# A hybrid encoder layer on one core: time steps finished in PSUM, attention outputs fetched earlier, two of eight gates kept in SBUF

## The chip, the core and the metric

The kernel runs on one core of a Trainium2 chip. A core has TensorE (PE in the profile; PEld is its loading of weights), VectorE (DVE), ScalarE (ACT), GpSimd (POOL) and SyncE (SP), which here only issues transfers. Each engine works off its own queue in order; they wait for each other by semaphores. SBUF is the working memory, PSUM holds the eight banks that TensorE writes. The metric is the device time of one execution in microseconds, the median of several; each comparison also has one profiled execution.

## The reference

One layer over 512 tokens of width 1024, float32. What the change touches is the token mixer:

```python
h = rmsnorm(x, pre_mix_norm[l])
proj = h @ w_in[l]                       # 1024 x 9792: z, x/B/C, dt, q, k, v, two gates
z, xbc, dt_raw, q, k, v, gates = split_cols(proj, IN_SPLITS)
# SSD branch, both directions, chunks of 128 tokens:
dt = softplus(dt_raw + dt_bias)          # time steps, 32 heads x 2 directions
a_dt = dt * -exp(a_log); a_cs = cumsum(a_dt) within the chunk
# ... scan with decays exp(a_cs), gated norm by groups, @ w_ssd_out -> y_ssd
# attention branch: +-128 tokens, 16 query heads on 4 key heads, sink logit, T5 bias
y_attn = window_attention(q, k, v, attn_sink[l], rel_bias_table) @ w_attn_out[l]
g = sigmoid(gates + b_gate)              # two gates, 1024 wide each
mixed = (g_ssd * y_ssd + g_attn * y_attn) @ w_o[l]
x = x + rmsnorm(mixed, post_mix_norm[l])
```

Behind it stands an MLP, 1024 to 4096 to 1024 with squared ReLU, with a norm ahead and behind, added to x.

## The kernel before

All of the activations lie transposed, 128 channels by 512 tokens. **Products.** A float32 matmul is made of three in the format float32r: every operand is split into a high part (ScalarE's copy, rounded) and a low part (the rest, a subtraction), and `mm3` sums high by high, high by low and low by high in one bank. A product of 128 columns of a weight matrix (`cm`) loads 512 KB of weights, splits them (line 538 on ScalarE, line 542 in three pieces on GpSimd) and issues 24 matmuls of 128x512. Three buffers each for raw weights, high and low parts stand ahead of TensorE. A product is called a quantum in the code; the list of quanta is the skeleton of the program, and everything else is hung on it: `self.at(q, fn)` says at which quantum `fn` is written out.

**Stages.** First the normed input h is made and split in 16 tiles (lines 758 to 761), v and dt come first, and `dt_math` (line 805 on) makes the time steps: softplus as a series on VectorE and ScalarE in one PSUM bank that holds two tiles, e and s2; line 828 writes the time steps `self.dt`, one of the tables in SBUF that the scan uses; line 830 multiplies them by -exp(a_log) into `al` (tile dtw). Three matmuls sum `al` along the chunk; all decays hang on these. Then nine rounds of input products (x, B, C, z, q and gates) stand between the scan of eight groups, with the sixteen attention heads spread over them. An attention output pair is scaled by VectorE (line 1006) and stored to DRAM (`spill`); so is each gate (`gate_quantum`, line 1043). In the last round the eight attention outputs are fetched (`attn_fetch`), split (`attn_split`, lines 1034 and 1035, the low parts in turn on VectorE and GpSimd) and multiplied by w_attn_out, eight products; each result is multiplied by its fetched gate (line 1051). The products by w_ssd_out, w_o and the MLP follow, from about 590 us to the end.

**Memory.** 83 slots of 128x512 in SBUF hold everything that is not weights. `Slots.get` takes the slot that has been free longest, `put` gives one back. Before the attention products the 16 tiles of h are given back, and the split of the attention outputs takes 16 slots then.

**The order.** When all is written out, `Planner` (line 117 on) makes each engine's order by a list schedule: it has a cost for every instruction (`duration`), a rule that VectorE with two wide SBUF operands and GpSimd hold each other off (`locks`, not for PSUM operands), a due time from the last instruction that needs the result (`deadlines`), and picks on each engine what is ready and due first. The engines' queues are then chained in that order. A small edit can so move instructions on all engines.

Of the kernel before, what the change touches and what calls it, by code (L numbers as in the profile page):

```python
# [14 lines left out]
ALU = mybir.AluOpType  # L15
# [48 lines left out]
            x_flip=1, b_flip=1, x_turn=1)  # L64
LAST = dict(SCAN, prep=(0, 1, 3, 4), outs=(2.5, 5.5), rms=8, finish=11)
FILLED, HEAD0, HEAD1 = "sfssfssfs", 1, -11
HEADS = dict(scores=0, flip=2, values=3.5)
BUCKET_STARTS = (1, 2, 3, 4, 5, 6, 7, 8, 12, 16, 23, 32, 46, 64, 91)

# [28 lines left out]
class Slots:  # L98
# [5 lines left out]
    def get(self, name, shape=(128, 512), dtype=F32):  # L104
        s = self.free.popleft()
        self.n += 1
        t = self.pool.tile(list(shape), dtype, tag=f"s{s}", name=f"{name}_{self.n}", bufs=1)
        self.tags[t.tensor.name] = f"s{s}", 1
        self.slot[id(t)] = (s, t)
        return t  # L110

    def put(self, *tiles):
        for t in tiles:
            self.free.append(self.slot.pop(id(t))[0])
# [287 lines left out]
class Trunk:  # L402
# [89 lines left out]
    def at(self, q, fn):  # L492

        self.acts.setdefault(max(q, self.now), []).append(fn)
# [310 lines left out]
    def dt_math(self):  # L805
        nc = self.nc
        get, put = self.slots.get, self.slots.put
        bias = self.row[:, :128].rearrange("p (i h) -> p i h", i=2)
        self.tables = [get("tables", (128, 2, 4, 64)) for _ in range(3)]
        self.ncs = self.tables[2][:, 0]  # L810
        self.dt, self.cs, self.dec, self.coef = (self.tables[i // 2][:, i % 2] for i in range(4))
        w = [self.dtv] + [get("dtw", (128, 4, 64)) for _ in range(3)]
        v, r, p, al = w
        bank = self.bank("ps")
        e, s2 = (bank[:, a:a + 256].rearrange("p (c h) -> p c h", c=4) for a in (0, 256))

        nc.scalar.activation(r, v, AF.Abs)
        nc.scalar.activation(e, r, AF.Exp, scale=-1.0)
        nc.scalar.activation(r, e, AF.Identity, bias=self.two)
        nc.vector.reciprocal(r, r)  # L820
        nc.vector.tensor_tensor(e, e, r, op=ALU.mult)
        nc.scalar.activation(s2, e, AF.Square)
        nc.scalar.activation(p, s2, AF.Copy, scale=1.0 / 17)
        nc.scalar.activation(v, v, AF.Relu)
        for n in (15, 13, 11, 9, 7, 5, 3):
            nc.vector.scalar_tensor_tensor(p, p, 1.0 / n, s2, op0=ALU.add, op1=ALU.mult)
        nc.vector.scalar_tensor_tensor(s2, p, 1.0, e, op0=ALU.add, op1=ALU.mult)
        nc.vector.scalar_tensor_tensor(self.dt, s2, 2.0, v, op0=ALU.mult, op1=ALU.add)
        nc.scalar.activation(bias[:, 1], bias[:, 1], AF.Exp)
        nc.vector.scalar_tensor_tensor(al, self.dt, -1.0, bias[:, 1].unsqueeze(1).to_broadcast([128, 4, 64]),  # L830
                                       op0=ALU.mult, op1=ALU.mult)

        def sums():
            pc = self.bank("ps")
            pc3 = pc[:, :256].rearrange("p (c h) -> p c h", c=4)
            self.mm(pc3[:, :, 0:32], self.U, al[:, :, 0:32], True, True)
            self.mm(pc3[:, :, 32:64], self.L, al[:, :, 32:64], True, True)
            pt = self.bank("ps")
            self.mm(pt[:, :256], self.ones, al, True, True)
            nc.vector.tensor_copy(self.cs, pc3)  # L840
            nc.scalar.activation(self.ncs, self.cs, AF.Copy, scale=-1.0)
            pt3 = pt[:, :256].rearrange("p (c h) -> p c h", c=4)
            nc.scalar.activation(self.dec, pt3, AF.Exp)
            nc.vector.tensor_tensor(self.coef, pt3, self.cs, op=ALU.subtract)
            nc.scalar.activation(self.coef, self.coef, AF.Exp)
            nc.vector.tensor_tensor(self.coef, self.coef, self.dt, op=ALU.mult)
            put(*w)

        def rows():
            px = self.bank("ps")  # L850
            for c in range(4):
                self.tr(px[:64, c * 128:(c + 1) * 128], self.cs[:, c, :])
            csr, cse = get("csr"), get("cse")
            nc.vector.tensor_copy(csr[:64], px[:64])
            nc.scalar.activation(cse[:64], px[:64], AF.Exp)
            self.csT = self.dp.tile([64, 512], F32, name="csT")
            self.csE = self.dp.tile([64, 512], F32, name="csE")
            chunks = lambda a: a.rearrange("p (c t) -> p c t", c=4)
            nc.sync.dma_start(self.inside(self.csT, 0, [128, 64], [8192, 4], [1, 128]), chunks(csr[:64]))
            for i in range(2):  # L860
                nc.sync.dma_start(self.inside(self.csE, 4096 * i, [128, 32], [8192, 4], [1, 128]), chunks(cse[i:64:2]))
            put(csr, cse)
            self.show("dt", self.dt)
            self.show("cs", self.cs)

        self.later(4, sums)
        self.later(5, rows)
# [154 lines left out]
        return t  # L1022

    def gate_fetch(self, m):
        self.gate[m] = self.fetch(self.gate[m], "gate")

    def attn_fetch(self):
        assert len(self.kept) == 8
        self.kept = [self.fetch(self.kept[k], "a") for k in range(8)]

    def attn_split(self):
        for k, a in enumerate(self.kept):
            hi, lo = self.slots.get("ah", dtype=F32R), self.slots.get("al", dtype=F32R)
            self.nc.scalar.copy(hi, a)
            (self.nc.vector if k % 2 == 0 else self.nc.gpsimd).tensor_tensor(lo, a, hi.bitcast(F32), op=ALU.subtract)
            self.slots.put(a)
            self.at_.append((hi, lo))

    def gate_quantum(self, m, dst):

        def done(ps):
            t = self.slots.get("gate")
            self.nc.scalar.activation(t, ps, AF.Tanh, bias=self.gbias(m), scale=0.5)  # L1043
            dst[m] = self.spill(t)

        return self.cm(self.d_w_in_b, C_GS - 64 + m * 128, lambda: self.h, done)

# [307 lines left out]
    def place_head(self, h, q):  # L1355

        at = lambda d: round(2 * (q + d)) / 2
        self.at(at(-2), lambda: self.attn_bias(h))
        self.at(at(HEADS["scores"]), lambda: self.attn_scores(h))
        self.at(at(HEADS["flip"]), lambda: self.attn_flip(h))  # L1360
        if h % 2:
            self.at(at(HEADS["values"]), lambda: self.attn_values(h // 2) if h // 2 in ALONE else self.due.append(h // 2))

# [461 lines left out]
    def build(self):  # L1825
# [4 lines left out]
        n = lambda: len(self.quanta)  # L1830
# [6 lines left out]
        for g in range(-1, 8):  # L1837
            q0 = n()
            if g < 7:
                f = deque(q[g + 3:g + 4] + ga[g + 1:g + 2] + gs[g + 1:g + 2])  # L1840
                p = deque(self.ssd_quanta(g + 1))
                for k in FILLED:
                    self.add(*[(p if k == "s" else f).popleft()] if k == "s" or f else [])
                if g < 0:
                    a0 = q0
                if g == 6:
                    for h in range(16):
                        self.place_head(h, a0 + HEAD0 + h * (n() + HEAD1 - a0 - HEAD0) / 15)
            else:
                self.at(n() - 4, self.attn_fetch)  # L1850
                self.at(n(), lambda: self.slots.put(*sum(self.h, ())))
                self.at(n(), self.attn_split)
                for m in range(8):
                    self.at(n() - 1, lambda m=m: self.gate_fetch(8 + m))
                    self.add(self.attn_out_quantum(m))
                for m in range(8):
                    self.at(n() - 2 + m // 2, lambda m=m: self.gate_fetch(MIX_ORDER[m]))
            if g >= 0:
                m = n() - q0
                self.place_ssd(g, lambda i, q0=q0, m=m: q0 + (min(i, m + 2) if g == 7 else round(i * m / 4) / 2 if 0 <= i <= 8 else m + i - 8 if i > 8 else i))  # L1860
# [47 lines left out]
```

## Time and profile before

| | us |
|---|---|
| runs, median (lowest to highest) | 1047.94 (1044.93 to 1048.61) |
| profiled execution, its own time | 1050.14 |
| its span, first to last instruction | 1048.4 |
| TensorE busy | 1035.3 |
| VectorE, GpSimd, ScalarE busy | 807.3, 730.0, 661.6 |

The profile's rows name a source line, an engine, an operation, and out<-in by the names of the tiles, with buffer numbers left out: `pp` and `ps` are PSUM banks, `wh` and `wl` the split weights, `h` the split input, `ah` and `al` the split attention outputs, `dtw` the tiles of the time steps' computation. In a timeline the two first numbers are the start and the duration in us, and brackets tell for how long the engine had been idle and what ended that. Matmuls overlap: one of 128x512 is shown as 0.39 long, and the next starts sooner. A table by stretches gives for each engine its busy time there, then the granted share of TensorE's clock, the busy share of the transfer engines and GB/s. Line numbers of the new file are one higher from line 67 on, two higher behind line 828, three behind 1026 and four behind 1850 (the scan's functions so stand three lines lower).

### The profile page before, as it was taken

Reading aid. Unit: us, or ns where it says so; the run is one execution under the profiler, and the core shown is the slowest. Engines: PE = TensorE matmul, PEld = TensorE weight load, DVE = VectorE, ACT = ScalarE, POOL = GpSimd, SP = SyncE. Lnnn points to the kernel's source line nnn. Section 1 sums busy time; section 2 is a strip of 40 time slices with the busy share of each in tenths; the row PEclk is TensorE's granted clock in tenths of the full one; section 3 lists DMA queues with packets and bytes.
Section 4 is the critical chain, followed back from the end, with each engine's and each line's share of the span. In section 5 each row is a group of like instructions: output and inputs, shape, how many; then the busy total and the mean of one; then the engine's idle time right before and its main releaser. Section 6 shows DMA issues by size and latency. Waiting matters only on the chain.

```text
span 1048.4 us, 16447 instructions
## 1 busy us (share of the span) xinstructions
PE 1035.3 (99%) x5298; PEld 867.9 (83%) x5298; DVE 807.3 (77%) x1371; ACT 661.6 (63%) x1393; POOL 730.0 (70%) x800
## 2 busy tenths in 40 slices
PE   9999999999999999999999999999999999999997
PEld 8788888888788888888878888889888888888886
DVE  6886987979989998896999546787853674584697
ACT  7776868775878787876877234656554444434553
POOL 5957567476585756748689655134688898898995
PEclk9999999999999999999999999999999999999999
DMA  8379989799799989999876734236222422424132
GB/s 309 114 185 243 228 233 202 178 224 226 190 243 232 238 178 236 252 228 237 227 205 213 254 124 138 97 110 205 88 89 83 141 81 89 153 80 161 61 101 81
DMA packets 151446, 182.27 MB, mean 174 GB/s; under 512 B 81976, under 2 KB 96312, under 8 KB 151360
## 3 DMA queue, kind: packets, MB, share of 16 engines
q1 hardware_dynamic: 151072, 180.92, 63.7%
q8 instruction: 42, 0.69, 0.3%
q14 instruction: 44, 0.36, 0.1%
q10 hardware_dynamic: 288, 0.30, 0.1%
HBM read 136.81 MB, written 27.59 MB: 157 GB/s over the span
## 4 chain that ended last, share of the span: by engine, by line
PE 47%; DVE 2%; ACT 1%; POOL 1%; DMA 1%; issue 1%; POOLq 0%; SPq 0%; DVEq 0%; ACTq 0%
PE pp L463 24%; PE ps L463 22%; DMA rstd<-rrow 1%; DVE yT L1345 0%; POOL wl L1693 0%; DVE x L1488 0%; DVE acc L1467 0%; POOL x L1819 0%; PE pp L467 0%; PE ps L467 0%; ACT wh L538 0%; DVE m L1240 0%; ACT yh L1388 0%; ACT th L1135 0%; POOL mrs L1481 0%
## 5 line engine op out<-in xcount | busy, mean ns | idle before, releaser
L542 POOL TENSOR_TENSOR wl<-wr,wh 128x342 fp32r<-128x342 f32 (+1 forms) x390 | 392.6, 1021 | 223.4 <-ACT wh L538 213.5
L463 PE MATMUL pp<-h,wh 128*128 128x512 f32 (+1 forms) x1664 | 505.7, 386 | 1.2 <-ACT gate L1043 0.9
L463 PEld LDWEIGHTS pp<-h,wh 128*128 128x128 f32 x1664 | 307.3, 188 | 62.2 <-issue 1.7
L463 PE MATMUL pp<-h,wl 128*128 128x512 f32 (+1 forms) x832 | 320.7, 386 | 0.0
L538 ACT CAST wh<-wr 128x1024 fp32r<-128x1024 f32 (+1 forms) x130 | 134.9, 1038 | 126.9 <-PE pp L463 94.9
L463 PEld LDWEIGHTS pp<-h,wl 128*128 128x128 f32 x832 | 156.8, 188 | 30.9 <-issue 0.2
L1693 POOL TENSOR_TENSOR wl<-wd,wh 128x256 fp32r<-128x256 f32 x158 | 133.4, 881 | 12.5 <-ACT wh L1690 12.1
L1690 ACT CAST wh<-wd 128x512 fp32r<-128x512 f32 x92 | 53.2, 618 | 36.3 <-PE ps L463 20.8
L463 PE MATMUL ps<-wl,fh 128*128 128x512 f32 x184 | 71.8, 390 | 0.2 <-POOL wl L1693 0.2
L463 PE MATMUL ps<-wh,fl 128*128 128x512 f32 x184 | 71.6, 389 | 0.0
L463 PE MATMUL ps<-wh,fh 128*128 128x512 f32 x184 | 71.6, 389 | 0.0
L1528 DVE SCALAR_TENSOR_TENSOR pp<-pp,r 128x256 f32<-128x256 f32 (+1 forms) x31 | 17.3, 558 | 66.7 <-ACT r L1525 66.5
L1237 ACT ACTIVATE n<-cb,tables 128x128 f32<-128x128 f32 x128 | 49.6, 391 | 17.7 <-DVE cb L1228 17.7
L1231 POOL TENSOR_TENSOR rb<-rb,tables 128x512 f32<-128x512 f32 x32 | 38.8, 1218 | 23.3 <-DMA rb<-csT 8.6
L1066 DVE SCALAR_TENSOR_TENSOR u<-pp,cv,u 128x510 f32<-128x510 f32 (+1 forms) x64 | 47.8, 747 | 3.3 <-ACT u L1062 2.0
L1238 ACT ACTIVATE m<-cb,tables 128x128 f32<-128x128 f32 x128 | 49.3, 389 | 0.0
L1233 ACT ACTIVATE rf<-rf,tables 128x128 f32<-128x128 f32 x128 | 41.5, 391 | 8.1 <-DMA rf<-csT 8.1
L463 PEld LDWEIGHTS ps<-wl,fh 128*128 128x128 f32 x184 | 34.5, 188 | 8.0 <-POOL wl L1693 0.6
L463 PEld LDWEIGHTS ps<-wh,fh 128*128 128x128 f32 x184 | 34.5, 188 | 7.2
L463 PEld LDWEIGHTS ps<-wh,fl 128*128 128x128 f32 x184 | 34.6, 188 | 7.1
L943 DVE COPY dp<-P 128x768 uint16<-128x768 uint16 (+1 forms) x48 | 39.7, 848 | 0.3
L973 ACT ACTIVATE P<-P,mx 128x256 f32<-128x256 f32 (+1 forms) x64 | 35.5, 557 | 7.0 <-DVE mx L965 6.8
(299 smaller groups left out, 2197.1 us busy)
## 6 DMA issues: line engine op xcount, KB each, us to landing
wr<-in_w_in_b SPq DMA_DIRECT2D x74, 512.0 KB, 5.2
wr<-in_w_mlp_in_b SPq DMA_DIRECT2D x32, 512.0 KB, 3.5
wd<-in_w_mlp_out SPq DMA_DIRECT2D x64, 256.0 KB, 5.3
zt<-dp SPq DMA_DIRECT2D x40, 256.0 KB, 5.2
rb<-csT SPq DMA_DIRECT2D x32, 256.0 KB, 5.5
rf<-csT SPq DMA_DIRECT2D x32, 256.0 KB, 5.5
wr<-in_w_ssd_out_b SPq DMA_DIRECT2D x13, 512.0 KB, 3.5
zt<-dp SPq DMA_DIRECT2D x32, 192.0 KB, 3.8
```

Of the source, the lines that this page charges most:

```text
L463: self.nc.tensor.matmul(out, lhsT, rhs, start=start, stop=stop, skip_group_check=more)
L538: self.nc.scalar.copy(hi[:, :m], raw)
L542: self.nc.gpsimd.tensor_tensor(lo[:, c], raw[:, c], hi[:, c].bitcast(F32), op=ALU.subtract)
L943: (copy or nc.vector.tensor_copy)(apart.rearrange("p (u k) -> p u k", u=2), src.bitcast(U16)[:, :2 * w].rearrange("p (k u) -> p u k", u=2))
L973: nc.scalar.activation(p[:, :w], p[:, :w], AF.Exp, bias=mx[:, n:n + 1], scale=-1.0, accum_out=sm[:, n:n + 1])
L1066: nc.vector.scalar_tensor_tensor(u[:, a:e], ps[:, a + d:e + d], self.wtap(t, b), u[:, a:e], op0=ALU.mult, op1=ALU.add)
L1231: nc.gpsimd.tensor_tensor(v4(rb), v4(rb), cs[:, 1].unsqueeze(2).to_broadcast([128, 4, 128]), op=ALU.subtract)
L1233: nc.scalar.activation(v4(rf)[:, h], v4(rf)[:, h], AF.Identity, bias=ncs[:, 0, h:h + 1])
L1237: nc.scalar.activation(v4(n)[:, h], cb[:, 0], AF.Copy, scale=dt[:, 0, h:h + 1])
L1238: nc.scalar.activation(v4(m)[:, h], cb[:, 1], AF.Copy, scale=dt[:, 1, h:h + 1])
L1690: nc.scalar.copy(hi, src)
L1693: (nc.vector if q == 512 else nc.gpsimd).tensor_tensor(lo[:, c], src[:, c], hi[:, c].bitcast(F32), op=ALU.subtract)
```

## The change

Three edits. **Time steps in the bank.** The last step of the softplus writes its result over s2 in the PSUM bank; the copy that the tables need is made by ScalarE (line 830 of the new file), and `al` is computed from s2 in PSUM (line 832). **Attention outputs.** They are fetched six products ahead of the first product that uses them, instead of four, and split in two halves, three products ahead and one, where all eight were split right at it. The 24 slots for this are taken while the 16 tiles of h are still held. **Gates.** Of each eight gates the last two (numbers 6, 7, 14 and 15) are neither stored nor fetched; they stay in the slots in which ScalarE made them.

```diff
+SPILLED = 6
@@ dt_math
-        nc.vector.scalar_tensor_tensor(self.dt, s2, 2.0, v, op0=ALU.mult, op1=ALU.add)
+        nc.vector.scalar_tensor_tensor(s2, s2, 2.0, v, op0=ALU.mult, op1=ALU.add)
+        nc.scalar.copy(self.dt, s2)
         nc.scalar.activation(bias[:, 1], bias[:, 1], AF.Exp)
-        nc.vector.scalar_tensor_tensor(al, self.dt, -1.0, bias[:, 1].unsqueeze(1).to_broadcast([128, 4, 64]),
+        nc.vector.scalar_tensor_tensor(al, s2, -1.0, bias[:, 1].unsqueeze(1).to_broadcast([128, 4, 64]),
                                        op0=ALU.mult, op1=ALU.mult)
@@
     def gate_fetch(self, m):
-        self.gate[m] = self.fetch(self.gate[m], "gate")
+        if m % 8 < SPILLED:
+            self.gate[m] = self.fetch(self.gate[m], "gate")
@@
-    def attn_split(self):
-        for k, a in enumerate(self.kept):
+    def attn_split(self, k0):
+        for k, a in enumerate(self.kept[k0:k0 + 4]):
@@ gate_quantum
-            dst[m] = self.spill(t)
+            dst[m] = self.spill(t) if m % 8 < SPILLED else t
@@ build
-                self.at(n() - 4, self.attn_fetch)
+                self.at(n() - 6, self.attn_fetch)
+                self.at(n() - 3, lambda: self.attn_split(0))
                 self.at(n(), lambda: self.slots.put(*sum(self.h, ())))
-                self.at(n(), self.attn_split)
+                self.at(n() - 1, lambda: self.attn_split(4))
```

The planner makes a new order from it. From the first half of the mixer to the last attention products (about 25 to 580 us) it differs on every engine in places; behind that no instruction changes its place. VectorE's queue around the end of the time steps, before (ps_363 is the bank, its wide inputs otherwise lie in SBUF):

```order
L880 TENSOR_TENSOR KL_515<-pp_487,KH_513 128x512
L827 SCALAR_TENSOR_TENSOR ps_363<-dtw_361,ps_363 128x256
L828 SCALAR_TENSOR_TENSOR tables_357<-ps_363,dtw_71 128x256
L830 SCALAR_TENSOR_TENSOR dtw_362<-tables_357,row 128x256
L906 SCALAR_TENSOR_TENSOR pp_533<-pp_533,rb_420 128x512
L915 TENSOR_TENSOR Q_559<-pp_533,Q_559 64x512
```

and now:

```order
L828 SCALAR_TENSOR_TENSOR ps_363<-dtw_361,ps_363 128x256
L882 TENSOR_TENSOR KL_516<-pp_488,KH_514 128x512
L829 SCALAR_TENSOR_TENSOR ps_363<-ps_363,dtw_71 128x256
L908 SCALAR_TENSOR_TENSOR pp_534<-pp_534,rb_421 128x512
L832 SCALAR_TENSOR_TENSOR dtw_362<-ps_363,row 128x256
L917 TENSOR_TENSOR Q_560<-pp_534,Q_560 64x512
```

The key split and the first scaling of a query bank have each traded places with a step of the time steps, and `al` (dtw_362) reads the bank. On TensorE the three sums of `al` stand one matmul sooner than before, ahead of the one that was the last in front of them.

VectorE's queue where the attention outputs are split, before (al is a low half of an attention output, yl one of the scan's output, sl of the squares for its norm):

```order
L1035 TENSOR_TENSOR al_6457<-a_6161,ah_6456 128x512
L1073 SCALAR_TENSOR_TENSOR C_6328<-th_6334,C_6328 128x512
L1035 TENSOR_TENSOR al_6465<-a_6165,ah_6464 128x512
L481 TENSOR_TENSOR sl_6313<-ssq_6303,sh_6312 128x512
L1138 SCALAR_TENSOR_TENSOR z_6382<-th_6384,pp_6357 128x2x128
L1035 TENSOR_TENSOR al_6473<-a_6169,ah_6472 128x512
L1138 SCALAR_TENSOR_TENSOR z_6383<-th_6384,pp_6357 128x2x128
L1138 SCALAR_TENSOR_TENSOR z_6382<-th_6444,pp_6405 128x2x128
L1138 SCALAR_TENSOR_TENSOR z_6383<-th_6444,pp_6405 128x2x128
L1389 TENSOR_TENSOR yl_6658<-yT_2130,yh_6657 128x512
```

and now:

```order
L1038 TENSOR_TENSOR al_6231<-a_6006,ah_6230 128x512
L1285 TENSOR_TENSOR w_5563<-ps_6301,z_5720 128x512
L1177 TENSOR_TENSOR xl_6357<-xd_6354,xh_6356 128x256
L1038 TENSOR_TENSOR al_6239<-a_6010,ah_6238 128x512
L1177 TENSOR_TENSOR xl_6363<-xd_6360,xh_6362 128x256
L1038 TENSOR_TENSOR al_6414<-a_6018,ah_6413 128x512
L1038 TENSOR_TENSOR al_6406<-a_6014,ah_6405 128x512
L482 TENSOR_TENSOR sl_6322<-ssq_6312,sh_6321 128x512
L1141 SCALAR_TENSOR_TENSOR z_6391<-th_6393,pp_6366 128x2x128
L1141 SCALAR_TENSOR_TENSOR z_6392<-th_6393,pp_6366 128x2x128
```

All four low halves that VectorE makes now stand together ahead of sl and of the products by z; before, three stood between these and the fourth fourteen places behind the third. SyncE's queue for the fetches, now:

```order
L1017 DMA sd_5881<-a_5879 128x512
L1023 DMA a_6006<-sd_1697 128x512
L1023 DMA a_6008<-sd_2237 128x512
L1023 DMA a_6010<-sd_3001 128x512
L1023 DMA a_6014<-sd_4065 128x512
L1023 DMA a_6018<-sd_5618 128x512
L519 DMA wr_6164<-in_w_in_b 128x1024
L1216 DMA rb_6424<-csT 128x512
L1023 DMA a_6020<-sd_5881 128x512
L1338 DMA rrow_5925<-rcol_5924 128x4
L1023 DMA a_6016<-sd_4829 128x512
L519 DMA wr_6222<-in_w_attn_out_b 128x1024
```

With one more that stands before these, six fetches are issued ahead of the last load of input weights (wr_6164) and all eight ahead of the first load of w_attn_out here; the last attention output is stored (sd_5881) right before its fellows are fetched.

## The prediction

> **What bounds the kernel now.** I read the page's first part, then the table by stage, then TensorE's own waits, and only then two places in time.
>
> ```profile
> PE 1035.3 (99%) x5298; PEld 867.9 (83%) x5298; DVE 807.3 (77%) x1371; ACT 661.6 (63%) x1393; POOL 730.0 (70%) x800
> ```
>
> ```profile
> core 0: us, PE busy (x) PEld busy (x) DVE busy (x) ACT busy (x) POOL busy (x), PEclk, DMA share, GB/s
> ...
> 600.00:650.00 50.00, 50.00 (x222) 41.43 (x221) 24.85 (x42) 16.00 (x23) 29.03 (x32) 1.00 0.39 128
> ```
>
> TensorE is the bound all through: from 600 us on it is never free (50.00 of 50), so whatever is saved before 600 us reaches the end undiminished, and nothing in the change lies behind that. What can be won is only what TensorE loses in waits and at a low clock. Its longest waits (total, times, longest):
>
> ```profile
> PE ps L463 <- DVE dtw L830: 2.0, 1, 2.0
> PE pp L463 <- DVE al L1035: 1.0, 1, 1.0
> PE pp L463 <- ACT gate L1043: 0.9, 1, 0.9
> ...
> PE ps L463 <- DVE w L1282: 0.3, 1, 0.3
> PE pp L463 <- DVE C L1066: 0.3, 1, 0.3
> PE ps L463 <- DVE mx L965: 0.3, 1, 0.3
> ```
>
> The two longest are the two that the change aims at: L830 makes the product of time step and decay rate (tile dtw, called al in the code), L1035 the low halves of the attention outputs (al).
>
> **Time steps in the bank.** The timeline of VectorE, GpSimd and TensorE at the first wait, and the clock there:
>
> ```profile
> 39.26 0.68 DVE L880 TENSOR_TENSOR KL<-pp,KH 128x512 fp32r<-128x512 f32 x1
> ...
> 40.77 6.23 DVE L830 SCALAR_TENSOR_TENSOR dtw<-tables,row 128x256 f32<-128x256 f32 x1
> 46.93 0.69 DVE L906 SCALAR_TENSOR_TENSOR pp<-pp,rb 128x512 f32<-128x512 f32 x1
> ```
>
> ```profile
> 39.35 3.56 POOL L761 TENSOR_TENSOR h<-xt,h 128x257 fp32r<-128x257 f32 x5
> 42.86 0.92 POOL L542 TENSOR_TENSOR wl<-wr,wh 128x342 fp32r<-128x342 f32 x1
> 43.73 2.13 POOL L761 TENSOR_TENSOR h<-xt,h 128x256 fp32r<-128x256 f32 x3
> 45.81 2.85 POOL L542 TENSOR_TENSOR wl<-wr,wh 128x341 fp32r<-128x341 f32 x3
> ```
>
> ```profile
> 44.65 0.39 PE L463 MATMUL pp<-h,wl 128*128 128x512 f32 x1
> 47.06 0.71 PE L463 MATMUL ps<-dtw,cst 128*128 128x128 f32 x4 [2.02 <-DVE dtw L830]
> ...
> 47.85 1.27 PE L463 MATMUL pp<-h,wh 128*128 128x512 f32 x2
> ...
> 52.38 0.28 PE L463 MATMUL ps<-KH,Q 128*128 128x256 f32 x1
> ```
>
> ```profile
> 44.00:47.00 3.00, 1.04 (x5) 0.54 (x3) 3.00 (x2) 0.00 (x0) 2.92 (x5) 1.00 0.51 175
> 47.00:48.50 1.50, 1.44 (x8) 1.28 (x9) 0.85 (x3) 0.83 (x2) 1.50 (x2) 0.84 0.00 0
> 48.50:51.40 2.90, 2.90 (x8) 2.33 (x7) 2.45 (x5) 2.80 (x5) 2.10 (x4) 0.50 0.53 172
> ```
>
> L830 took 6.23 us. Both its wide operands lie in SBUF, and GpSimd works on SBUF without a pause beside it. That GpSimd is the cause is told by the group ahead of it: L826 is of the same form and size, ran beside a GpSimd that was as busy, but with one operand in PSUM, and seven times it took no more than 423 ns (its duration here as min/median/max, in the first row):
>
> ```profile
> L826 DVE SCALAR_TENSOR_TENSOR dtw<-dtw,ps x7: 421/422/423, 36.2 to 38.9; 128x256 f32<-128x256 f32 x7
> L1035 DVE TENSOR_TENSOR al<-a,ah x4: 683/876/1411, 527.1 to 545.4; 128x512 fp32r<-128x512 f32 x4
> ```
>
> The change gives L830 (L832 in the new file) a PSUM operand, so I price it at 0.42. When is it done? The last L826 starts at 38.9 and ends at 39.3. Behind them the new order puts the closing product (0.42), a key split (L880, 0.68), the time step (0.42), the scaling of a query bank (L906, 0.69) and then this one (0.42): 2.63, so about 42.0 us. TensorE asks for it where it now issues the matmul at 44.65. It is there over 2 us early, and the wait is gone.
>
> What it is worth: before, the score matmuls start at 52.38. Without the wait there stand, after 44.65, one matmul (0.23), the sums (0.80, from 47.06 to 47.85), twelve matmuls of 0.227 (2.72; the stage from 600 us has 222 in 50.00 us, 0.225, and the last two rows of the fence on the attention outputs stand 0.23 apart), and two changes of number format for which I allow 0.3: 48.70. Gain 3.7, in 3.4 to 4.0. About 2.0 of it is the wait and the rest the half clock behind it (0.50 for 2.9 us, 0.84 for 1.5: 1.45 + 0.24 = 1.7 us).
>
> What comes next in line? GpSimd is no slower than before: its low halves of h end at 43.73 + 2.13 = 45.86, and the last is asked for at about 48; its weight piece ends at 48.66, of which the first third (46.7) is asked for at about 50.3. ScalarE gets one more instruction, the copy of the time steps to SBUF:
>
> ```profile
> 47.65 0.58 ACT L914 CAST Q<-pp 64x512 fp32r<-64x512 f32 x1 [5.06 <-DVE pp L906]
> ...
> 52.43 0.38 ACT L843 ACTIVATE tables<-ps 128x256 f32<-128x256 f32 x1
> ```
>
> An instruction of its size from PSUM took 0.38, and ScalarE sat idle for 5.06 us here behind the same late VectorE: I put it at nothing. If the idle time were gone, the query casts would be 0.4 later; the query bank is scaled by 41.6, so even then they are some 6 us ahead of the scores at 48.7.
>
> [...] The row first: L830 lost 5.8 us to about eight GpSimd instructions, while every other VectorE instruction in that position (the second row above, 683 alone and 1411 at most) lost no more than one. [...]
>
> **Attention outputs.** The second wait, in TensorE's and VectorE's timelines:
>
> ```profile
> 528.93 0.39 PE L463 MATMUL pp<-ah,wh 128*128 128x512 f32 x1
> ...
> 531.97 0.39 PE L463 MATMUL pp<-ah,wh 128*128 128x512 f32 x1
> 533.36 0.50 PE L463 MATMUL pp<-al,wh 128*128 128x512 f32 x1 [1.00 <-DVE al L1035]
> ...
> 535.32 0.39 PE L463 MATMUL pp<-ah,wl 128*128 128x512 f32 x1
> 535.55 0.39 PE L463 MATMUL pp<-al,wh 128*128 128x512 f32 x1
> ```
>
> ```profile
> 529.24 1.41 DVE L1035 TENSOR_TENSOR al<-a,ah 128x512 fp32r<-128x512 f32 x1
> 530.58 1.41 DVE L481 TENSOR_TENSOR sl<-ssq,sh 128x512 fp32r<-128x512 f32 x1
> 531.90 0.41 DVE L1138 SCALAR_TENSOR_TENSOR z<-th,pp 128x256 f32<-128x256 f32 x1
> 532.24 1.07 DVE L1035 TENSOR_TENSOR al<-a,ah 128x512 fp32r<-128x512 f32 x1
> ```
>
> From 528.93 to 535.55 start 23 matmuls: 22 distances of 0.227 are 4.99, and it took 6.62. So 1.6 us are lost, because VectorE makes each low half only when TensorE already stands before it. In the new order (rows in the section on the change) all four of VectorE's low halves stand ahead of the y splits and ahead of the ssq split that came between. I take 1.3 of 1.6; the bounds are 1.6 (all) and 0 (the four only trade places with scan work, for which TensorE then waits). The data is no matter: the last fetch was issued at 506.92, 20 us before its use.
>
> ```profile
> 506.92 0.39 SPq L1021 DMA_DIRECT2D a<-sd  x1
> ```
>
> **Fetches earlier, four gates less.** Two products of 24 matmuls are 10.9 us, so eight fetches of 256 KB (2.1 MB) move from the second of these stretches toward the first, and eight transfers of the same size (four spills, four fetches) fall away, the spills mostly in the first:
>
> ```profile
> 449.00:499.00 50.00, 49.95 (x328) 42.60 (x327) 39.15 (x70) 36.20 (x83) 34.07 (x37) 1.00 0.97 234
> 499.00:549.00 50.00, 48.74 (x240) 39.35 (x239) 46.82 (x67) 40.02 (x84) 39.59 (x37) 1.00 0.77 217
> ```
>
> ```profile
> wr<-in_w_in_b SPq DMA_DIRECT2D x74, 512.0 KB, 5.2
> ```
>
> At 234 GB/s the moved 2.1 MB are 9.0 us of transfer, the spills 4.5 less. A weight load lands in 5.2 us (the last row) and three weight buffers hold it two products (10.9) ahead: 5.7 us of cover against 4.5. I put the whole at nothing, bounds 0 and 3.3 (9.0 less 5.7).
>
> **The rest of the order.** The planner moves scan work on all engines up to about 580 us. TensorE's other waits there (gate 0.9; w, C and mx 0.3 each) are 1.8 us; a new order may lose them or find as many. Among what it may find are waits for memory: 24 slots are taken while h holds 16, so scan tiles get slots that were given back more lately. I take 0, bounds 1.8 either way.
>
> **Sum.** 3.7 + 1.3 = 5.0 us. The profiled execution took 1050.14 (span 1048.4), so 1045.1 there; the median of the runs is 2.2 lower, 1047.94, so 1042.9.
>
> **Rivals.**
> 1. The half clock is not in the timed runs. For: the profiled execution is 1.5 us slower than the slowest timed run, about the clock's price. Against: clock and wait stand side by side in the only trace. Then 2.0 + 1.3: 1044.6. [...]
> 2. The attention wait stays: VectorE is 46.82 of 50 busy there, and a split that comes earlier pushes scan work. 3.7 alone: 1044.2.
> 3. The re-planned order also loses the small waits: 3.7 + 1.3 + 1.8 = 6.8: 1041.1.
> 4. L830's 6.23 us is not GpSimd's doing, but for instance the broadcast row operand, which stays. By the row 421/422/423 less likely. Only 1.3: 1046.6. [...]
> 5. Slower: SyncE's queue is in order, and the last input weights and the first attention weights now stand behind six and eight fetches. If nothing covers them, TensorE stops for 9.0 and runs 1.7 longer at half clock: +10.7 - 3.7 = +7.0: 1054.9. It decides once such a load lands over 5.7 us late. Against: the four gates' traffic is gone from the same queue.
>
> **How the numbers follow.** Forecast 0.49, rival 1 0.14, 2 0.11, 3 0.16, 4 0.06, 5 0.04. 0.5% is 5.2 us here, about what can be told from no change, and the bound is 1042.7, close to the forecast: of its 0.49, which spreads over 1041.1 to 1044.7 with the unknown order, I count 0.25 below and 0.24 above. Faster: 0.25 + 0.16 = 0.41. Slower: 0.04. Same: the rest, 0.55. The range reaches from rival 3 with all bounds at their best (4.0 + 1.6 + 1.8 = 7.4, 1040.5) to rival 4 (1046.6), each with some 0.5 more for the spread of a median: 1040.0 to 1047.2.
>
> **What would show it.** Right: L832 takes about 0.42 us; no TensorE wait on dtw; the clock 1.00 from 44 to 52; the first score matmul near 48.7; 23 matmuls of the first attention product within 5.3 us; the end 5 us sooner with TensorE still 50.00 of 50 from 600 us. Wrong: L832 still long; half clock elsewhere; a wait on al, on a weight load or on scan work between 480 and 580 us that was not there.

## The result: 0.37% faster, at the time that was forecast, but not from where it was forecast

| | us |
|---|---|
| forecast | 1042.9 (1040.0 to 1047.2) |
| after, median of 7 runs (lowest to highest) | 1042.79 (1040.58 to 1043.83) |
| before, beside it, 7 runs | 1046.54 (1044.85 to 1048.61) |
| ratio, 95% interval | 0.9963 (0.9947 to 0.9978) |
| after, profiled execution (its span) | 1043.74 (1042.0) |

The page's first part of the changed kernel, and all the waits that TensorE has in it (total, times, longest):

```profile
PE 1032.8 (99%) x5298; PEld 868.6 (83%) x5298; DVE 794.0 (76%) x1371; ACT 662.4 (64%) x1394; POOL 728.8 (70%) x800
```

```profile
PE ps L464 <- ACT xh L1176: 1.1, 1, 1.1
PE pp L464 <- PEq L1900: 0.8, 1, 0.8
PE ps L464 <- DVE xl L1177: 0.5, 1, 0.5
```

That is within 0.5%, the likeliest of the three cases by the forecast. The gain, 3.75 us, is three quarters of the 5.0 that were forecast. The waits on the time steps, on the attention halves and on the gate are gone (those on the time steps and the gate are missing from the second profile of the kernel before as well, further down); the waits on the scan's x halves (xh, xl) are 1.6 us where they were 0.4. At the time steps everything stands as forecast. VectorE's and TensorE's timelines there, and the table by stretches:

```profile
40.05 0.69 DVE L908 SCALAR_TENSOR_TENSOR pp<-pp,rb 128x512 f32<-128x512 f32 x1
41.14 0.42 DVE L832 SCALAR_TENSOR_TENSOR dtw<-ps,row 128x256 f32<-128x256 f32 x1 [0.39 <-ACT tables L830]
```

```profile
48.83 0.28 PE L464 MATMUL ps<-KH,Q 128*128 128x256 f32 x1
...
411.93 0.39 PE L464 MATMUL ps<-xh,bt 128*128 128x256 f32 x1 [1.08 <-ACT xh L1176]
412.81 0.39 PE L464 MATMUL ps<-xl,bt 128*128 128x256 f32 x1 [0.49 <-DVE xl L1177]
```

```profile
48.50:51.40 2.90, 2.90 (x18) 2.55 (x17) 2.42 (x9) 1.92 (x4) 2.82 (x5) 1.00 0.49 177
...
410.00:414.00 4.00, 2.43 (x13) 1.65 (x12) 3.13 (x5) 2.99 (x6) 4.00 (x7) 1.00 1.00 377
414.00:417.50 3.50, 3.50 (x11) 2.73 (x10) 2.86 (x4) 2.99 (x9) 3.42 (x4) 0.51 1.12 218
```

L832 took 0.42 and ended at 41.56, the clock behind it is 1.00, and the first score matmul stands at 48.83. But a new stop with a new half clock stands at 410 to 417.5.

To see where time goes I take, from each trace, the distance from each matmul's start to the next, less the distance that its shape has at full clock (0.227 us for 128x512, the median in the first profiles of both kernels), and add it up by stretches. The sums differ as the spans do (24.0 less 17.6 is 6.4; 1048.4 less 1042.0 too). The table holds the runs below as well; ratios stand against the kernel before, run beside each. Three executions far outside the rest are left out of medians and ratios: 1145.48 us of the kernel before, 1295.24 of split late and 2111.17 of al from SBUF, which is that kernel's profiled one, so that its trace is not used.

| lost by TensorE, us, from .. to | 0-25 | 25-75 | 75-300 | 300-475 | 475-600 | 600- | sum | ratio of the runs (95%) |
|---|---|---|---|---|---|---|---|---|
| before | 3.4 | 4.4 | 6.0 | 4.4 | 4.4 | 1.4 | 24.0 | |
| before, again | 4.4 | 0.6 | 4.9 | 4.0 | 5.6 | 1.4 | 20.8 | 1.0016 (1.0004-1.0027) |
| three halves up | 3.8 | 0.5 | 4.6 | 3.2 | 6.5 | 1.4 | 20.0 | 1.0028 (1.0016-1.0039) |
| attention alone | 4.5 | 0.6 | 4.9 | 3.2 | 5.1 | 1.4 | 19.6 | 1.0006 (0.9993-1.0020) |
| gates alone | 4.0 | 0.5 | 4.5 | 3.8 | 4.6 | 0.9 | 18.3 | 0.9987 (0.9974-1.0000) |
| split late | 4.0 | 0.6 | 3.9 | 3.3 | 3.7 | 1.0 | 16.4 | 0.9988 (0.9975-1.0002) |
| all but time steps | 4.7 | 0.6 | 4.6 | 3.3 | 3.0 | 0.9 | 17.1 | 0.9964 (0.9950-0.9977) |
| time steps and gates | 3.5 | 0.5 | 4.0 | 8.4 | 2.8 | 1.0 | 20.2 | 0.9975 (0.9962-0.9988) |
| time steps alone | 3.7 | 0.6 | 4.9 | 5.5 | 1.8 | 1.0 | 17.4 | 0.9953 (0.9936-0.9969) |
| after | 3.4 | 0.9 | 3.9 | 6.3 | 2.2 | 0.9 | 17.6 | 0.9963 (0.9947-0.9978) |
| after, again | 4.1 | 0.6 | 4.0 | 4.0 | 2.2 | 0.9 | 15.8 | 0.9963 (0.9948-0.9977) |

Two things are to be seen. The 4.4 us at the time steps stand in one row alone, the first profile of the kernel before. And of the columns only the one from 475 to 600 us, with the attention products, goes nearly as the ratios go.

### The profile page after: what moved, and what is told of

It is laid out like the page before. It is cut to its first block, busy times and chain, and to the rows that moved or that the text cites. A ratio compares the mean times of both kernels' runs of the same rounds, so it can differ in the third digit from the quotient of the medians.

```text
span 1042.0 us, 16422 instructions
## 1 busy us (share of the span) xinstructions
PE 1032.8 (99%) x5298; PEld 868.6 (83%) x5298; DVE 794.0 (76%) x1371; ACT 662.4 (64%) x1394; POOL 728.8 (70%) x800
## 4 chain that ended last, share of the span: by engine, by line
PE 96%; DVE 1%; DMA 1%; ACT 1%; issue 1%; POOL 0%; POOLq 0%; ACTq 0%
PE pp L464 63%; PE ps L464 33%; DMA rf<-csT 1%; PE ps L468 0%; DVE x L1491 0%; DVE acc L1470 0%; POOL x L1822 0%; PE pp L468 0%; DVE rf L1237 0%; DVE C L1076 0%; ACT P L975 0%; POOL mrs L1484 0%; DVE xl L1177 0%; DVE P L967 0%; POOLq L1908 0%
```

## Experiments

### What holds VectorE off beside GpSimd

A program of its own: GpSimd makes 14 subtractions of 128x256 without a pause, VectorE one instruction beside them, in five kinds, two times each (A, B, C and the row in SBUF, P in PSUM).

```diff
+    if kind == "flat":      stt(out, A, -1.0, B, op0=ALU.mult, op1=ALU.mult)
+    elif kind == "repeat":  stt(v4(out), v4(A), -1.0, wide, op0=ALU.mult, op1=ALU.mult)
+    elif kind == "bank":    stt(v4(out), v4(P), -1.0, wide, op0=ALU.mult, op1=ALU.mult)
...
```

> A kernel of its own that leaves the whole layer out and writes zeros: GpSimd runs 14 subtractions of 128x256 in SBUF without a pause (0.74 us each in the layer), and after the third VectorE gets one 128x256 instruction: two flat SBUF operands; the same with one operand a 64-wide row repeated four times; a PSUM operand with that repeated row; two operands in four pieces of 64; a plain multiplication with the repeated row; then all five once more. If it is the port that GpSimd and VectorE share, with one GpSimd instruction's wait at most: all but the PSUM one take 0.45 to 1.2 us, the PSUM one 0.42. If a VectorE instruction can starve behind any run of GpSimd without a pause: all four with two SBUF operands take until the run ends, 6 us or more, the PSUM one 0.42. If it is the repeated row that starves: only the two SBUF ones with the row are long; if the pieces do it, the one in pieces as well.

Durations in ns, as min/median/max:

```profile
L24 DVE SCALAR_TENSOR_TENSOR out<-A,B x2: 803/803/803, 14.0 to 67.9; 128x256 f32<-128x256 f32 x2
L26 DVE SCALAR_TENSOR_TENSOR out<-A,row x2: 800/801/802, 24.8 to 78.7; 128x256 f32<-128x256 f32 x2
L28 DVE SCALAR_TENSOR_TENSOR out<-P,row x2: 424/424/424, 35.8 to 89.6; 128x256 f32<-128x256 f32 x2
```

With two SBUF operands it took 0.80 us, 0.38 more than the 0.42 with one of them in PSUM; the repeated row is no matter (0.80 with it and without). The two other kinds, operands in pieces of 64 and a plain product with the row, have two SBUF operands and took 0.80 as well. So the place of the operands decides here beside GpSimd, but for 0.38 us, about half of one GpSimd subtraction (0.74 in the layer), not for 5.8. The shared port of the expectation is a guess at the cause; the runs show the time alone.

### Each edit alone, and all but one

Time steps alone (the change's lines in `dt_math`, with `al` from s2):

```diff
-        nc.vector.scalar_tensor_tensor(self.dt, s2, 2.0, v, op0=ALU.mult, op1=ALU.add)
+        nc.vector.scalar_tensor_tensor(s2, s2, 2.0, v, op0=ALU.mult, op1=ALU.add)
+        nc.scalar.copy(self.dt, s2)
...
```

> Only the time steps in the bank. Port theory: the product of time step and decay takes 0.42 us, no TensorE wait on it, 3.7 us less than before where the half clock follows that wait in the timed runs (ratio 0.9965), 2.0 where it does not (0.9981). Rival, that the gain of the whole change comes from the re-planned order or from the attention outputs: ratio 0.999 to 1.001 even with that instruction short.

1042.65 us (6 runs), ratio 0.9953 (0.9936 to 0.9969). That is as fast as the 0.9965 of the port theory or faster; the next runs do not bear out its reason.

Attention outputs alone:

```diff
-                self.at(n() - 4, self.attn_fetch)
+                self.at(n() - 6, self.attn_fetch)
+                self.at(n() - 3, lambda: self.attn_split(0))
...
-                self.at(n(), self.attn_split)
+                self.at(n() - 1, lambda: self.attn_split(4))
```

> Only the attention outputs' fetch and split moved; all gates are stored and fetched as before, the time steps as before. My theory: TensorE's wait on al goes, 1.3 us less (ratio 0.9988), the wait on dtw of 2.0 us stays. Rival, that the split only pushes scan work: 0 or slower (1.000 to 1.002), with a new wait between 480 and 560 us.

1048.47 us (12 runs), ratio 1.0006 (0.9993 to 1.0020). The wait on al that this edit was to take away still stands in its trace:

```profile
PE pp L464 <- DVE al L1037: 1.4, 1, 1.4
```

The halves came earlier only in part: ScalarE's last high half starts at 530.9, 7.3 us behind the first matmul that uses such halves (523.6).

The change without its time-step edit (`al` is made from `self.dt` again):

```diff
-        nc.vector.scalar_tensor_tensor(s2, s2, 2.0, v, op0=ALU.mult, op1=ALU.add)
-        nc.scalar.copy(self.dt, s2)
+        nc.vector.scalar_tensor_tensor(self.dt, s2, 2.0, v, op0=ALU.mult, op1=ALU.add)
...
```

> The whole change without its first part. Port theory: the wait on dtw of some 2.0 us is back, and 2.0 to 3.7 us of the gain of 3.75 are lost: ratio 0.998 to 1.000. Rival, that the first part is worth little in the timed runs: it stays at 0.9963.

1044.06 us (6 runs), ratio 0.9964 (0.9950 to 0.9977): the rival on record, not the 2.0 to 3.7 us that were to be lost. Its trace has no wait on al.

The edits do not add up: the time steps alone win as much as all, all without them win nearly the same, and the attention edit alone wins nothing. Where the old line for `al` stands it ran beside GpSimd again, in the trace of attention alone and of all but time steps:

```profile
L831 DVE SCALAR_TENSOR_TENSOR dtw<-tables,row 128x256 f32<-128x256 f32 x1 | 0.9, 907 | 0.0
```

```profile
L831 DVE SCALAR_TENSOR_TENSOR dtw<-tables,row 128x256 f32<-128x256 f32 x1 | 0.9, 902 | 0.0
```

With both operands in SBUF it took 0.91 and 0.90 us there, not 6.23, and nothing waited for it. So the next run was the kernel before itself.

### Both kernels again, the gates alone, and al from SBUF

The kernel before, with no edit:

> The kernel before, unchanged, for a second profiled execution and for the spread of a kernel against itself. Theory A (the prediction's): VectorE's instruction for al with both wide operands in SBUF is held off by GpSimd in every execution: about 6.2 us again, TensorE waits 2.0 us for it, half a clock behind it, TensorE loses some 4.4 us between 25 and 75 us. Theory B (chance): in the two kernels that kept the old lines and whose traces we have, the same instruction took 0.90 and 0.91 us; then the 6.23 us were an accident of one execution: 0.9 us here, no wait on dtw, under 0.6 us lost between 25 and 75 us, and a profiled time near the timed median, 1045 to 1048. The ratio to the kernel before is 1.000 within 0.002 by both.

VectorE's group at L830, TensorE's longest waits, and the stretch that had half the clock in the first profile:

```profile
L830 DVE SCALAR_TENSOR_TENSOR dtw<-tables,row 128x256 f32<-128x256 f32 x1 | 0.9, 907 | 0.0
```

```profile
PE pp L463 <- DVE al L1035: 2.5, 2, 1.6
PE ps L463 <- DVE m L1240: 1.0, 1, 1.0
```

```profile
48.50:51.40 2.90, 2.90 (x18) 2.56 (x17) 2.42 (x7) 2.23 (x5) 2.82 (x4) 1.00 0.42 127
```

Theory B holds: 0.907 us, no wait on dtw, clock 1.00. The old line took 0.90 to 0.91 in five executions (this one, attention alone, all but time steps and, below, gates alone and three halves up) and 6.23 in one. The kernel took 1048.15 us here (12 runs) beside 1047.02 of itself (35 runs); the ratio, 1.0016 (1.0004 to 1.0027), leaves out 1, so two sets of runs of one program differ by more than the interval knows. Below some 0.2% I therefore call nothing shown.

The changed kernel, with no edit:

> The changed kernel, unchanged, on the same chip as the others here, with a second profiled execution. By both theories 0.42 us for al, and a ratio near 0.996 (1042 to 1044). What it tells apart is the 2 us stop of TensorE at 410 to 413 us (two waits for the high and low halves of x in the scan): if it belongs to the new order it stands here again with 1.9 to 2.0 us, if it was chance it is under 0.5 us. Half a clock behind it for 3.4 us: in the first profile yes, in the time-steps-only kernel no with the same stop; so either is possible here, and it is worth 1.7 us.

1042.35 us (12 runs), ratio 0.9963 (0.9948 to 0.9977). The stop at 411 us was 0.5 us here where it was 1.6, and no half clock stands behind it.

The gates alone:

```diff
-        self.gate[m] = self.fetch(self.gate[m], "gate")
+        if m % 8 < SPILLED:
+            self.gate[m] = self.fetch(self.gate[m], "gate")
...
-            dst[m] = self.spill(t)
+            dst[m] = self.spill(t) if m % 8 < SPILLED else t
```

> The kernel before with only the gates' edit (two of eight neither stored nor fetched). Prediction: nothing to be had, ratio 1.000 within 0.0015, 1046.5 to 1048.5. Rival: the kernel with all edits but the time steps was 4.4 us below the one with the attention edit alone, and the gates are the only difference: then this one is at 1043 to 1044.5, ratio 0.996. Third: the gain comes from whatever new order falls out: anything between 1041 and 1048, with a different set of small waits in the stretches from 200 to 475 us.

1045.15 us (12 runs), ratio 0.9987 (0.9974 to 1.0000): not told apart from nothing, and not the 4 us of the rival. L831 took 0.905 here, and a wait on al of 1.4 us stands in the trace.

The changed kernel with `al` from SBUF:

```diff
-        nc.vector.scalar_tensor_tensor(al, s2, -1.0, bias[:, 1].unsqueeze(1).to_broadcast([128, 4, 64]),
+        nc.vector.scalar_tensor_tensor(al, self.dt, -1.0, bias[:, 1].unsqueeze(1).to_broadcast([128, 4, 64]),
```

> The changed kernel, but al computed from ScalarE's copy of the time steps in SBUF, so both wide operands lie in SBUF again. If the PSUM operand is what the time-steps edit is worth (prediction): 3 to 4 us slower than the changed kernel, 1046 to 1047, al over 5 us long and a TensorE wait on it. If the hold-off is one GpSimd instruction as everywhere else: al 0.8 to 1.0 us, no wait on dtw, and a time within 1 us of the changed kernel, but for what the re-planned order makes.

1043.55 us (11 runs), ratio 0.9970 (0.9956 to 0.9984), beside 0.9963 for the change on the same chip. By these two the operand in PSUM, the core of the time-step edit, is worth 0.7 us; with their intervals that is anything from 1.4 us the other way to 2.8, so it is not told from nothing, and it falls short of the 3 to 4 us expected. No trace shows how long al took in this kernel.

### Three instructions moved, and nothing else

In the second profile of the kernel before, VectorE's and TensorE's timelines at the first attention product:

```profile
518.63 3.40 DVE L1345 SCALAR_TENSOR_TENSOR yT<-w,cv,rstd 128x256 f32<-128x256 f32 x4 [2.18 <-DMA rstd<-rrow]
...
523.40 0.68 DVE L1035 TENSOR_TENSOR al<-a,ah 128x512 fp32r<-128x512 f32 x1
...
526.10 1.39 DVE L1035 TENSOR_TENSOR al<-a,ah 128x512 fp32r<-128x512 f32 x1
...
529.07 1.07 DVE L1035 TENSOR_TENSOR al<-a,ah 128x512 fp32r<-128x512 f32 x1
```

```profile
527.54 0.50 PE L463 MATMUL pp<-al,wh 128*128 128x512 f32 x1 [1.55 <-DVE al L1035]
...
530.20 0.50 PE L463 MATMUL pp<-al,wh 128*128 128x512 f32 x1 [0.99 <-DVE al L1035]
```

VectorE stood idle for 2.18 us because the product at the head of its queue (yT) waited for a transfer, with low halves behind it that lacked nothing. So I left the planner's order as it was and put three low halves ahead of that product:

```diff
-        for order in plan.plan().values():
+        orders = plan.plan()
+        o = orders["DVE"]
...
+        halves = [o[k] for k in (727, 722, 724)]
+        o[716:728] = halves + [n for n in o[716:728] if n not in halves]
+        for order in orders.values():
```

> The kernel before in its own order, but for three instructions: VectorE's first three low halves of the attention outputs stand ahead of the four products L1345 that wait for a transfer (rstd), not behind them. In the second profile of the kernel before VectorE sat idle there for 2.2 us with the data of all three ready, and TensorE then waited 1.6 and 1.0 us for two of them; that stretch (475 to 600 us) lost 5.6 us. Theory (the place of these instructions decides, whichever edit moves them): no TensorE wait on al in the first product, 2.5 to 3 us lost in that stretch, the time 2 to 3.5 us below the kernel before, 1043.5 to 1045, ratio 0.997 to 0.998. Rival (VectorE is simply full there and the delay goes on to the scan): another wait of 2 to 3 us in its place, on C or yl, and a ratio of 1.000 within 0.0015.

1047.74 us (12 runs), ratio 1.0028 (1.0016 to 1.0039): not faster, and beside the kernel's 1.0016 to itself not shown to be slower. VectorE's, ScalarE's and TensorE's timelines:

```profile
514.70 3.05 DVE L1041 TENSOR_TENSOR al<-a,ah 128x512 fp32r<-128x512 f32 x3
```

```profile
526.98 1.06 ACT L1141 ACTIVATE th<-pp 128x512 f32<-128x512 f32 x2
527.95 0.61 ACT L1394 CAST yh<-yT 128x512 fp32r<-128x512 f32 x1
528.46 0.62 ACT L1040 CAST ah<-a 128x512 fp32r<-128x512 f32 x1
```

```profile
529.13 0.72 PE L463 MATMUL pp<-ah,wh 128*128 128x512 f32 x2 [2.17 <-ACT ah L1040]
```

The three low halves are done 5.6 us ahead of the product (at 517.7; it starts at 523.3). The four yT took 4.03 us instead of 3.40, and C, which VectorE makes behind them, cost TensorE 0.9 us of wait in all instead of 0.3. And TensorE now stands for 2.17 us for a high half that ScalarE makes behind other work: the next late one in line, just as late. The wait on VectorE was the one that showed, not the only one. My theory, that the place of VectorE's halves decides, falls; of the rival's two signs, the wait in another place came (2.17 us, on ah and not on C or yl), the ratio within 0.0015 of 1 did not.

### Without the attention edit, and with its splits late

The change without its attention edit:

```diff
-                self.at(n() - 6, self.attn_fetch)
-                self.at(n() - 3, lambda: self.attn_split(0))
+                self.at(n() - 4, self.attn_fetch)
...
-                self.at(n() - 1, lambda: self.attn_split(4))
+                self.at(n(), self.attn_split)
```

> The change without its attention edit (time steps and gates only; the fetch four ahead and all splits at the first product, as before). If the attention edit is worth its 1.3 us beside the others: 1043.5 to 1045, with a TensorE wait on al. If what counts is only where the planner happens to put VectorE's low halves: as the time-steps-only kernel, 1041 to 1043.5 and no wait on al, or, with another draw, up to 1046 with one; the wait in the trace and the time go together.

1042.42 us (12 runs), ratio 0.9975 (0.9962 to 0.9988), and no wait on al in its trace: beside the other two edits the attention edit is not told from nothing. The profiled execution, 1046.4 us, was one of its two longest. TensorE's waits and the clock there:

```profile
PE ps L464 <- ACT xh L1176: 1.8, 2, 1.5
PE ps L464 <- DVE sl L482: 1.0, 1, 1.0
```

```profile
410.00:414.50 4.50, 1.53 (x5) 0.56 (x3) 4.12 (x7) 1.94 (x5) 4.50 (x6) 1.00 1.02 370
414.50:418.00 3.50, 3.42 (x11) 2.92 (x12) 2.44 (x4) 3.05 (x8) 3.45 (x4) 0.56 0.91 181
```

This is the stop of the changed kernel at 411 us, larger: TensorE worked for 1.53 of 4.50 us and then had half the clock.

The change with its splits written out at the first product:

```diff
-                self.at(n() - 3, lambda: self.attn_split(0))
+                self.at(n(), lambda: self.attn_split(0))
...
-                self.at(n() - 1, lambda: self.attn_split(4))
+                self.at(n(), lambda: self.attn_split(4))
```

> The change with both halves of the split written out at the first product again (fetches stay six ahead, gates and time steps as changed). Prediction: the split's place is what saves the attention wait, so a wait on al of about 1 us and 1 to 2 us more than the change, 1043.5 to 1045. Rival: the planner, which orders by due time, puts the low halves as early as in the change; no wait on al, 1041.5 to 1043.5.

1044.48 us (11 runs), ratio 0.9988 (0.9975 to 1.0002); no wait on al, but the stretch from 475 to 600 us lost 3.7 us against 2.2. That is 1.5 us for the early split, but one planned order against another: without the whole attention edit (time steps and gates, above) the same stretch lost 2.8. When the halves are made fits it in part. ScalarE's high halves (durations, then the first and last start) in the second profile of the kernel before, and of the change:

```profile
L1034 ACT CAST ah<-a x8: 602/620/630, 507.2 to 538.8; 128x512 fp32r<-128x512 f32 x8
```

```profile
L1037 ACT CAST ah<-a x8: 602/618/630, 501.6 to 523.3; 128x512 fp32r<-128x512 f32 x8
```

The first product's first matmul starts at 524.2 before: the last high half starts 14.6 us behind it. After, it starts at 523.5, and the last high half 0.2 us ahead. With the splits late it is 8.8 us behind again (530.9, 522.1). In the time-steps-only kernel the last one starts at 535.0, 9.9 us behind the first matmul, and still nothing waits: there the planner has spread that product out among other matmuls. Orders without the wait, then, come with the attention edit and without it, and attention alone shows that the edit does not secure one.

### The moment of asking

> The layer is left out; zeros are written. Sixty times GpSimd makes ten subtractions of 128x256 or 128x257 (0.74 us each, each waiting for its own cast by ScalarE, float32r out), and VectorE puts one instruction with two SBUF operands (one a repeated row, as L830) beside them, each time 12 ns later. Theory: VectorE can lose several turns when it asks at an unlucky moment: most take 0.42 to 1.2 us, a few at one or two starts take over 2 us. Rival: it never loses more than one turn: none above 1.2 us, and the one 6.23 us stays without an explanation.

The layer is replaced by this loop; `n` moves the moment at which VectorE asks:

```diff
+        for k in range(RUN):
+            w = 256 + k % 2
+            c = slice(k * WIDE, k * WIDE + w)
+            nc.scalar.copy(hi[:, c], x[:, c])
+            nc.gpsimd.tensor_tensor(lo[:, c], x[:, c], hi[:, c].bitcast(F32), op=ALU.subtract)
...
+        n = 16 + 12 * step
+        nc.vector.tensor_copy(Q[:, :min(n, 400)], P[:, :min(n, 400)])
...
+        nc.vector.scalar_tensor_tensor(v4(res), v4(A), -1.0, row.unsqueeze(1).to_broadcast([128, 4, 64]),
+                                       op0=ALU.mult, op1=ALU.mult)
```

```profile
L50 DVE SCALAR_TENSOR_TENSOR res<-A,row x60: 412/538/1032, 8.9 to 514.3; 128x256 f32<-128x256 f32 x60
```

Sixty times, none above 1.03 us: at most 0.62 above the shortest (0.41), less than one GpSimd instruction (0.74). Wherever it was held off in this loop, it ended 0.28 us behind the instruction that held it; asking in the last 0.14 us of a GpSimd instruction it lost nothing, but for once (1.03, with 0.07 us left), when the next one went first. The moments tried include the one of the 6.23 us (19 ns into a GpSimd instruction; 16 and 22 ns here). So the rival holds, and what made that one execution take 6.23 us stays open.

## Why the number was right and the reasons were not

**The time: two errors that cancel.** The forecast took 5.0 us off 1047.94, the median of three runs. The seven runs beside the change have 1046.54, 1.4 us less, and the gain was 3.75, 1.25 less. That 1042.79 stands 0.1 from the forecast is luck.

**Time steps, 3.7 us: an event of one execution, taken for the kernel.** What it cost was sized well: from the matmul ahead of the sums to the first score matmul it took 7.73 us (44.65 to 52.38) in the first profile and 3.84 (45.67 to 49.51) in the second, 3.9 us less with nothing changed. The 0.3 us that the forecast allowed there for two changes of number format were an estimate, which no run shows as a term: with them the forecast's terms sum to 4.05, where the second profile has the 3.84. But of six executions of that line five show 0.90 to 0.91. The step that failed is the last of the sum: 5.0 was taken off the profiled execution (1050.14), and then off the median as well. The median did not hold those 3.7 us, by all that the runs tell: the first profiled execution lay 3.6 above the median of the seven runs, just the price of the event, and the second, without it, took 1046.93, at the median of 35 (1047.02). The forecast had seen 2.2 above its own median and 1.5 above the slowest timed run, and had counted that for rival 1, as the price of the half clock alone, where it spoke for the whole event.

**What the other row said.** In the same profile L1035, with two SBUF operands as well, took at most 1.41 us where its shortest took 0.68: 0.73 more, where L830 took 5.8 more. Five other executions of L830 and sixty of the loop lost no more than L1035 (0.90 to 0.91, and 1.03 at most, over 0.41). So the 6.23 us were an exception, to be explained before they were counted. The forecast saw that row, gave another cause 0.06 as rival 4, and went by the single execution. That GpSimd is the one who holds off, which rival 4 denied, is shown for 0.38 us (0.80 with SBUF operands, 0.42 with PSUM), not for the 6.23 us; in the five other executions TensorE did not wait for it.

**Attention outputs, 1.3 us: right in kind, too small.** Between the second profiles the stretch from 475 to 600 us lost 5.6 before and 2.2 after, 3.4 us less; between the first ones 2.2 less. The forecast counted the wait on VectorE's low halves alone. The run with three halves moved shows that ScalarE's high halves are as late; the change makes both earlier, and this may be why it wins more than the wait that the page of the profile names. It is not shown: time steps alone lost least there, 1.8, with its high halves late. The bound "all of 1.6" was no bound: it was read from one execution of a wait that was 1.0 in one profile and 2.5 in the next.

**Fetches and gates at nothing.** No run of either edit is shown to be slower, rival 5 did not come, and the gates alone are not told from nothing. With the time steps left out the two edits together give 0.9964, though: there the gates and the attention edit made an order in which the gain appears, as the time steps did alone.

**The re-planned order, 0 with 1.8 either way: too narrow.** Time steps alone take 0.47% (0.31 to 0.64), some 5 us, with an operand whose own worth is not told from nothing. What they brought, as far as these runs tell, is another order. The new order also has the stop at 411 us, of 0.5 to 1.6 us in the two profiles of the change, 1.5 in that of the time steps alone and 3.1 in time steps and gates. Two of the twelve later runs of the changed kernel (1046.2 and 1046.5) lie some 4 us above their median; whether they had this stop with a half clock behind it cannot be told, since they have no trace.

**What stays open.** The column from 475 to 600 us goes with the ratios over nine kernels, and the five traces that lost 4.4 us or more in it are the five in which TensorE waits for a half of the attention outputs (al, with three halves up ah). But each kernel is a different order, and the one run that changed three places alone did not gain; that this stretch is the cause of the whole 4 us is so argued, not shown. Between the second profiles 3.4 of the 5.0 us lie in it, 0.9 between 75 and 300, 0.5 behind 600, 0.3 at the start. No version here is told apart from the change as faster: time steps alone, 0.9953, has an interval that holds 0.9963.

## What to carry to other kernels

A wait in one profile is a sample. Before its price is taken off a median, look whether the profiled execution lies above the timed runs by about that price, and take a second profile. And where a planner writes the order, an edit's own worth and the worth of the order that it sets off are two things: test the edit with the order kept, and count, behind a late operand, the one that is late next.

## What the hardware showed beside that

**The half clock stands on a grid in three traces.** In three of the eleven traces of the layer that are used the clock fell in mid-kernel, each time for 3.413 us. From the first moment of full clock to the fall it was 44.373 us in the first profile of before (13 times 3.413) and 409.599 in the change and in time steps and gates (120 times). Laid on that grid, the stretches with most idle TensorE time are those below, without the start-up, without the stretches that had half clock themselves, and without the last ones, which hold almost no matmul (2.87 us idle and more, all followed by half clock). Idle time is given as the profile draws matmuls, and by distances, where a matmul counts only for the distance that its shape has at full clock (0.227 us for 128x512, 0.12 for 128x256, medians of the first profiles of both kernels), as in the table of losses:

| kernel | stretch of 3.413 us, from | idle, as drawn, us | idle, by distances, us | clock in the next stretch |
|---|---|---|---|---|
| time steps and gates | 411.54 | 2.16 | 2.79 | 0.50 |
| three halves up | 1036.68 | 2.31 | 2.47 | 0.50 |
| before | 44.60 | 2.02 | 2.39 | 0.50 |
| after, again | 1032.17 | 2.00 | 2.16 | 0.50 |
| after | 410.61 | 1.57 | 2.13 | 0.50 |
| gates alone | 1034.55 | 1.86 | 2.10 | 1.00 |
| time steps alone | 1033.46 | 1.65 | 1.99 | 1.00 |
| time steps and gates | 1036.18 | 1.55 | 1.90 | 1.00 |
| attention alone | 528.37 | 1.46 | 1.84 | 1.00 |
| all but time steps | 1032.89 | 1.44 | 1.79 | 1.00 |
| three halves up | 528.09 | 1.45 | 1.75 | 1.00 |
| before, again | 524.12 | 1.54 | 1.70 | 1.00 |
| time steps alone | 412.23 | 1.15 | 1.54 | 1.00 |

As drawn, idle time does not tell the two apart: 1.57 us was followed by half clock, 1.65 and 1.86 were not. By distances it does: all five stretches with 2.13 us or more were followed by half clock, none of those with 2.10 or less; that margin is too narrow to call the border measured. In the rows from mid-kernel the half clock lasted 3.413 us, so the stop before it cost 1.7 us more, half of that. The wait of 2.17 us with three halves up was cut by a border of the grid as laid (1.13 and 1.04 as drawn; the rest of the row is another wait) and cost nothing more; the stop of time steps alone, at the same place as the change's, was cut too. In the three traces the borders count from the moment at which the clock comes up, 3.6, 4.4 and 5.4 us into the execution (before, the change, time steps and gates). If they do so in every execution, the same stop can cost more in one execution of a kernel than in another; no two executions of one kernel here show that.
